# Layer 0's x in a two-layer encoder: turned by PE from its rows, or loaded again in 32-wide blocks and turned by DVE

## The chip, the cores and the metric

The kernel runs on one core of one Trainium2 chip. The metric is the device time of one execution in microseconds. Before the change three runs took 962.6 to 963.75 us, median 963.07. The core has a matrix engine (PE, TensorE), which needs the stationary operand of a product with the contracted index on its 128 partitions; a vector engine (DVE), a scalar engine (ACT), a general engine (POOL), and SP, which here only issues transfers. The transfers run on 16 DMA engines.

## The reference, cut to what matters

x has 256 rows (positions) of 2048 numbers, mem has 256 rows (memory tokens) of 2048. There are two layers. All numbers are float32.

```python
for l in range(2):
    h = rmsnorm(x, norm_g[l])
    proj = h @ w_in[l]                    # 2048 x 7168: gated conv, differential attention, memory attention
    ...
    mn = rmsnorm(mem, mem_norm_g[l])
    mkv = mn @ w_mem_kv[l]                # 2048 x 1024: keys and values of 256 memory tokens
    ...
    y = concatenate([y_a, y_d, y_m], axis=-1) @ w_out[l]    # 2048 x 2048
    x = x + y
```

`rmsnorm` divides a row by the root of its mean square and multiplies by a gain for each of the 2048 columns. The kernel leaves the division to the end of a product (a row's factor can be applied to the result) and applies only the gain to the operand.

## The kernel before, in words

**Products.** `block` computes 256 rows by 512 columns of a product. It walks over the contracted index in 16 slices `k` of 128, two slices to a step. Both operands are split into a leading part and a remainder (`hi` and `lo`), and three products are summed: lines 237, 238 and 239, for each of two row tiles `t`. So a block is 16 x 2 x 3 = 96 matmuls of 128x512. There are 40 blocks: two memory blocks (keys, values) a layer, 14 of `w_in` a layer, 4 of `w_out` a layer.

**Weights.** `load_w` (called by `block` for each step) has SP load two slices of weights, 512 KB, into one of four `raw` buffers (line 210). ACT makes `hi` (line 218, or 221 with a gain) and DVE the remainder `lo` (219, 222), each into one of eight buffers. So weights can be ahead of PE by up to eight slices as `hi` and `lo`, and four more loads as `raw`.

**Operands.** The stationary operand of a block is kept turned, as a tile of 128 partitions by 2 parts by 16 slices by 256 positions. `memT` is the turned mem; `xT` the turned x with the layer's gain. `rows_T` makes two slices at a time: four turns of 128x128 on PE against an identity (line 495; two slices by two row tiles), and `split_T` then has ACT write the leading part (line 200, with the gain as its scale) and DVE the remainder (line 201). `x_rows` is a generator that does this for all 16 slices in eight pieces.

**Order.** The blocks run in this order: memory keys of layer 0, memory values of layer 0, memory keys of layer 1, memory values of layer 1, then the layers themselves. While a block runs, `run_side` takes one piece of side work from a queue of generators after each step. A planner then lays out each engine's instructions from their dependencies and the order in the program; an instruction wrapped in `keep_in_program_order` is held behind whatever its own engine was given before it. Loads of weights and constants are not held in that way.

mem and x share one buffer, `xs`, of rows as they stand in memory. mem is loaded first, and turned while the first block runs (`mem_piece`). During the second block `mem_square` is called before each step's weight load: it takes sums of squares of mem for the row factors, and loads the small constants, among them the gains `norm_g`, which are turned into the columns of `cvb` at its fifth step. In the third block `x_load` brings x into `xs`, 256 columns ahead of each weight load (line 549). In the fourth block `x_rows(xT, 0, ...)` is on the side queue and turns x. The first projection block of layer 0 follows, and needs `xT`. In layer 1, x has been computed on the chip and `x_rows` turns it in the same way.

The pool `keep` has one buffer for each tag; the tags `v`, `ga`, `bgx`, `bgT`, `mqT` and `mga` hold tiles that the layers write later.

Of the kernel before, what the change touches and what calls it, by code (L numbers as in the profile page):

```python
# [10 lines left out]
F32 = mybir.dt.float32  # L11
# [3 lines left out]
ALU = mybir.AluOpType  # L15
# [3 lines left out]
P = 128  # L19
# [4 lines left out]
KT = D_MODEL // P  # L24
# [19 lines left out]
def encoder(ctx: ExitStack, tc: tile.TileContext, x, mem, norm_g, w_in, conv_w, conv_b,  # L44
            dq_g, dk_g, lq1, lk1, lq2, lk2, head_g, mem_norm_g, w_mem_kv, mq_g, mk_g, w_out, out):
    nc = tc.nc
    x, mem, out = x[0], mem[0], out[0]

    def pool(name, bufs, space=None):
        kw = {"space": space} if space is not None else {}  # L50
        return ctx.enter_context(tc.tile_pool(name=name, bufs=bufs, **kw))
# [4 lines left out]
    keep = pool("keep", 1)  # L56
# [8 lines left out]
    def nm(s):  # L65
        uid[0] += 1
        return f"{s}_{uid[0]}"
# [20 lines left out]
    def on_all_rows(v):  # L88
        return v.rearrange("l d -> (l d)").unsqueeze(0).to_broadcast([P, DEPTH * HALF])
# [3 lines left out]
    def load_constants(part):  # L93
        if part is None:
            return
        if part == 0:
            for j, v in enumerate((lq1, lk1, lq2, lk2)):
                nc.sync.dma_start(lam_in[:, j, :], on_all_rows(v))
        else:
            for r0, v in vb_rows[(part - 1) * 4:part * 4]:  # L100
                n, w = v.shape
                for j in range(P // w):
                    nc.sync.dma_start(vb[r0:r0 + n, j * w:(j + 1) * w], v)
# [16 lines left out]
    def g_norm(l, k):  # L120
        return cvb[:, 64 + l * KT + k:65 + l * KT + k]

    def g_mnorm(l, k):
        return cva[:, l * KT + k:l * KT + k + 1]

    cvb = const.tile([P, 96], F32, name="cvb")
# [26 lines left out]
    def rsqrt(t, n):  # L153

        y = small.tile([P, n], F32, tag=f"rs_y{n}", name=nm("rsy"))
        a = small.tile([P, n], F32, tag=f"rs_a{n}", name=nm("rsa"))
        yi = y.bitcast(I32)
        nc.vector.tensor_scalar(yi, t.bitcast(I32), 1, None, ALU.logical_shift_right)
        nc.vector.tensor_scalar(yi, yi, -1.0, float(0x5F3759DF), ALU.mult, ALU.add)
        for _ in range(3):  # L160
            nc.vector.scalar_tensor_tensor(a, y, -0.5, y, ALU.mult, ALU.mult)
            nc.vector.tensor_tensor(a, a, t, ALU.mult)
            nc.vector.scalar_tensor_tensor(y, a, 1.5, y, ALU.add, ALU.mult)
        return y

    side = deque()
# [126 lines left out]
    def col(st, which, t):  # L293
        return st[:, which, t:t + 1]

    def normed(acc, gs, st):

        ng = NB // gs
        ss = small.tile([P, NT, ng], F32, tag=f"ss{ng}", name=nm("ss"))
        for t in range(NT):  # L300
            sq = tmp.tile([P, NB], F32, tag="nat", name=nm("sq"), bufs=4)
            nc.scalar.activation(sq, acc[t], AF.Square)
            nc.vector.tensor_reduce(ss[:, t], sq.rearrange("p (g d) -> p g d", d=gs), AX.X, ALU.add)
            nc.vector.tensor_scalar(ss[:, t], ss[:, t], col(st, R2_64 if gs == HALF else R2_128, t), EPS,
                                    ALU.mult, ALU.add)
        r = rsqrt(ss.rearrange("p t g -> p (t g)"), NT * ng).rearrange("p (t g) -> p t g", t=NT)
        res = []
        for t in range(NT):
            nc.vector.tensor_scalar(r[:, t], r[:, t], col(st, R, t), None, ALU.mult)
            y = tmp.tile([P, NB], F32, tag="nat", name=nm("nat"), bufs=4)  # L310
            nc.vector.tensor_tensor(y.rearrange("p (g d) -> p g d", d=gs),
                                    acc[t].rearrange("p (g d) -> p g d", d=gs),
                                    r[:, t].unsqueeze(2).to_broadcast([P, ng, gs]), ALU.mult)
            res.append(y)
        return res

    def turn(nat, dests):


        for t in range(NT):  # L320
            pt = ps_t.tile([P, NB], F32, tag="t", name=nm("pt"))
            for j in range(NB // P):
                nc.tensor.transpose(pt[:, j * P:(j + 1) * P], nat[t][:, j * P:(j + 1) * P], ident)  # L323
            at = 0
            for dst, h0, nh, gain in dests:
                nc.scalar.activation(dst[:, h0:h0 + nh, t * P:(t + 1) * P],
                                     pt[:, at * P:(at + nh) * P].rearrange("p (h q) -> p h q", h=nh),
                                     AF.Copy, scale=gain)
                at += nh
            yield  # L330
# [159 lines left out]
    def rows_T(dst, src, k, gain=None, n=2):  # L490

        pt = ps_t.tile([P, 2, SEQ], F32, tag="t", name=nm("pt"))
        for j in range(n):
            for t in range(NT):
                nc.tensor.transpose(pt[:, j, t * P:(t + 1) * P], src(k + j, t), ident)  # L495
        for j in range(n):
            split_T(dst, k + j, pt[:, j, :], None if gain is None else gain(k + j))

    def x_rows(dst, l, ks):
        for k in ks:  # L500
            rows_T(dst, lambda k, t: xs[:, t, k * P:(k + 1) * P], k, lambda k: g_norm(l, k))
            yield

    def stats_of(parts, tag):
        ss = small.tile([P, NT], F32, tag="ssum", name=nm("ssum"))
        nc.vector.tensor_reduce(ss, parts, AX.X, ALU.add)
        return row_stats(ss, tag)

    def T_tile(what):
        return big.tile([P, 2, KT, SEQ], F32R, tag="T", name=nm(what))  # L510
# [3 lines left out]
    def x_square(c, t):  # L514
        sq = tmp.tile([P, NB], F32, tag="nat", name=nm("sq"), bufs=4)
        nc.scalar.activation(sq, xs[:, t, c * NB:(c + 1) * NB], AF.Square, accum_out=ssx[:, t, c:c + 1])
# [13 lines left out]

    def mem_square(k):

        load_constants((1, 2, 0, None)[k // 2] if k < 8 else None)
        if k == 8:
            rest_of_constants()
        if k < 8:
            c = k // 2
            for t in range(NT):
                sq = tmp.tile([P, NB], F32, tag="nat", name=nm("sq"), bufs=4)
                tc.keep_in_program_order(  # L540
                    nc.scalar.activation(sq, xs[:, t, c * NB:(c + 1) * NB], AF.Square, accum_out=ssm[:, t, c:c + 1]))

        if k == 10:
            stm.append(stats_of(ssm, "stm"))
            side.append(turn(normed(acc_k, P, stm[0]), [(mkT[0], 0, MH, cvb[:, 56:57])]))

    def x_load(k):
        tc.keep_in_program_order(
            nc.sync.dma_start(xs[:, :, k * P:(k + 2) * P],
                              x[:, k * P:(k + 2) * P].rearrange("(t p) c -> p t c", p=P)))  # L550

    mkT, mv, stm = [], [], []
    for l in range(DEPTH):
        mkT.append(keep.tile([P, MH, SEQ], F32, tag=f"mkT{l}", name=f"mkT{l}"))
        mv.append(keep.tile([P, NT, W_MEM], F32, tag=f"mv{l}", name=f"mv{l}"))
        gm = lambda k: g_mnorm(l, k)
        pinned[0] = l == 0
        acc_k = block(memT, w_mem_kv[l], [(0, NB)], ALLK, gain=gm, before=mem_piece if l == 0 else x_load)
        pinned[0] = False
        if l > 0:  # L560
            side.append(turn(normed(acc_k, P, stm[0]), [(mkT[l], 0, MH, cvb[:, 56 + l:57 + l])]))
            xT = T_tile("xT")
            side.append(x_rows(xT, 0, range(0, KT, 2)))
        acc = block(memT, w_mem_kv[l], [(W_MEM, NB)], ALLK, gain=gm, before=mem_square if l == 0 else None)
        for t in range(NT):
            nc.scalar.activation(mv[l][:, t, :], acc[t], AF.Copy, scale=col(stm[0], R, t))  # L566
    for c in range(4):
        for t in range(NT):
            x_square(c, t)
    flush_side()  # L570

    for l in range(DEPTH):
# [5 lines left out]
        v = keep.tile([P, NT, W_DIFF], F32, tag="v", name=nm("v"))  # L578
        ga = keep.tile([P, NT, W_DIFF], F32, tag="ga", name=nm("ga"))
# [19 lines left out]
        mqT = keep.tile([P, MH, SEQ], F32, tag="mqT", name=nm("mqT"))  # L599
        mga = keep.tile([P, NT, W_MEM], F32, tag="mga", name=nm("mga"))  # L600
# [11 lines left out]
        bgT = None  # L612
# [67 lines left out]
        if l + 1 < DEPTH:  # L680
            xT = T_tile("xT")
# [47 lines left out]
```

## Time and profile before

| | us |
|---|---|
| median of three runs | 963.07 |
| the profiled execution's own time | 962.88 |
| its span | 961.1 |
| PE busy | 953.7 |
| DVE busy | 671.6 |
| ACT busy | 560.6 |

The span is the time from the first to the last instruction. Busy times are sums over an engine's instructions within the span; matmuls are pipelined, so one shows some 0.39 us although they follow one another closer than that. PEld is the load of the stationary operand, which runs beside the matmuls. A row of the lines view gives the line, the engine, the operation, the tiles and their shape, the count, the busy time and mean in ns, and then the idle time before it with what ended it. A row of a window gives for each engine the busy time and count, then the clock of PE as granted (1.00 is full), the mean busy share of the 16 DMA engines, and GB/s. A row of a timeline gives the start, the time to the end of the row's instructions, and what they are; x4 means four merged. The chain of waits gives start, time and what the end of the program hung on at that moment. In the DMA view a line gives packets and bytes of a stretch, and a queue's line the packets, the MB and the time of its packets as a share of 16 engines' time in that stretch.

### The profile page before, as it was taken

The numbers are of one execution on the slowest core, as the hardware profiler recorded it, in microseconds if no ns is written. First come the engines' busy times: TensorE is split into PE (matmuls) and PEld (weight loads), VectorE is DVE, ScalarE is ACT, GpSimd is POOL, SyncE is SP. The second block draws the span as 40 slices with busy tenths as digits, with TensorE's granted clock in tenths as the row PEclk, the third lists the DMA queues.
The fourth block names the chain that finished last, engine by engine and source line by source line (L and its number), as shares of the span: only waits on it lengthen the run. The fifth ranks groups of instructions, "written<-read, shape, count | busy, mean of one in ns | idle before, by whom it ended". The sixth has DMA issues, their size and how long they took to land.

```text
span 961.1 us, 13428 instructions
## 1 busy us (share of the span) xinstructions
PE 953.7 (99%) x4482; PEld 790.4 (82%) x4482; DVE 671.6 (70%) x1496; ACT 560.6 (58%) x1103; POOL 1.4 (0%) x8
## 2 busy tenths in 40 slices
PE   8999999999999999999999999999999999999998
PEld 6888888888888888888888888888888888888886
DVE  5867778865787775567666678856787775568562
ACT  5857656755666655554555556754665655554441
POOL 0000000000000000000000000000000000000000
PEclk9999999999999999999999999999999999999999
DMA  8775565566555555555555665576455555555661
GB/s 267 263 270 181 171 195 178 167 209 195 175 154 167 166 165 161 176 172 178 177 188 184 188 184 177 175 213 194 147 170 176 162 169 165 174 168 176 216 227 58
DMA packets 103530, 175.27 MB, mean 182 GB/s; under 512 B 6318, under 2 KB 29732, under 8 KB 103460
## 3 DMA queue, kind: packets, MB, share of 16 engines
q1 hardware_dynamic: 102116, 173.09, 57.5%
q10 hardware_dynamic: 1344, 1.33, 0.5%
q8 instruction: 35, 0.57, 0.2%
q14 instruction: 35, 0.29, 0.1%
HBM read 172.29 MB, written 2.10 MB: 181 GB/s over the span
## 4 chain that ended last, share of the span: by engine, by line
PE 98%; DMA 1%; DVE 0%; SPq 0%; ACT 0%; issue 0%; DVEq 0%; ACTq 0%
PE acc L237 30%; PE acc L239 30%; PE acc L238 30%; PE po L357 2%; PE pt L495 1%; PE ptT L350 1%; PE s L465 1%; DMA xs<-in_mem_dram 1%; PE s L419 1%; PE s L418 1%; PE ptq L383 1%; PE py L342 0%; PE pt L323 0%; PE pt L638 0%; PE pt L629 0%; DVE lo L222 0%
## 5 line engine op out<-in xcount | busy, mean ns | idle before, releaser
L218 ACT CAST hi<-raw 128x512 fp32r<-128x512 f32 x576 | 355.9, 622 | 318.3 <-PE acc L239 195.3
L219 DVE TENSOR_TENSOR lo<-raw,hi 128x512 fp32r<-128x512 f32 x576 | 394.9, 689 | 203.8 <-ACT hi L218 198.7
L237 PE MATMUL acc<-hi,xT 128*128 128x512 f32 x896 | 353.9, 395 | 0.0
L238 PE MATMUL acc<-lo,xT 128*128 128x512 f32 x896 | 352.2, 393 | 0.0
L239 PE MATMUL acc<-hi,xT 128*128 128x512 f32 x896 | 350.3, 393 | 0.0
L237 PEld LDWEIGHTS acc<-hi,xT 128*128 128x128 f32 x896 | 168.4, 188 | 33.8
L238 PEld LDWEIGHTS acc<-lo,xT 128*128 128x128 f32 x896 | 168.4, 188 | 33.5
L239 PEld LDWEIGHTS acc<-hi,xT 128*128 128x128 f32 x896 | 168.0, 188 | 33.6
L238 PE MATMUL acc<-lo,yT 128*128 128x512 f32 x256 | 99.9, 391 | 0.0
L239 PE MATMUL acc<-hi,yT 128*128 128x512 f32 x256 | 99.2, 390 | 0.0
L237 PE MATMUL acc<-hi,yT 128*128 128x512 f32 x256 | 98.3, 392 | 0.0
L222 DVE SCALAR_TENSOR_TENSOR lo<-raw,cva,hi 128x512 fp32r<-128x512 f32 x64 | 46.2, 748 | 16.2 <-ACT hi L221 15.8
L239 PEld LDWEIGHTS acc<-hi,yT 128*128 128x128 f32 x256 | 48.1, 188 | 9.9
L238 PEld LDWEIGHTS acc<-lo,yT 128*128 128x128 f32 x256 | 48.1, 188 | 9.8
L237 PEld LDWEIGHTS acc<-hi,yT 128*128 128x128 f32 x256 | 48.1, 188 | 9.7
L221 ACT ACTIVATE hi<-raw,cva 128x512 fp32r<-128x512 f32 x64 | 44.0, 721 | 19.4 <-PE acc L239 10.6
L238 PE MATMUL acc<-lo,memT 128*128 128x512 f32 x124 | 48.6, 392 | 0.0
L239 PE MATMUL acc<-hi,memT 128*128 128x512 f32 x124 | 48.4, 390 | 0.0
L237 PE MATMUL acc<-hi,memT 128*128 128x512 f32 x124 | 44.5, 395 | 0.1
L238 PEld LDWEIGHTS acc<-lo,memT 128*128 128x128 f32 x124 | 23.3, 188 | 4.9
L239 PEld LDWEIGHTS acc<-hi,memT 128*128 128x128 f32 x124 | 23.3, 188 | 4.8
L237 PEld LDWEIGHTS acc<-hi,memT 128*128 128x128 f32 x124 | 22.8, 188 | 5.0 <-ACT mv L566 0.5
(154 smaller groups left out, 686.9 us busy)
## 6 DMA issues: line engine op xcount, KB each, us to landing
raw<-in_w_in_dram SPq DMA_DIRECT2D x192, 512.0 KB
raw<-in_w_out_dram SPq DMA_DIRECT2D x64, 512.0 KB
raw<-in_w_in_dram SPq DMA_DIRECT2D x64, 256.0 KB
raw<-in_w_mem_kv_dram SPq DMA_DIRECT2D x31, 512.0 KB
xs<-in_x_dram SPq DMA_DIRECT2D x8, 256.0 KB
xs<-in_mem_dram SPq DMA_DIRECT2D x7, 256.0 KB
out_dram<-xs SPq DMA_DIRECT2D x8, 128.0 KB
out_dram<-xs ACTq DMA_DIRECT2D x8, 128.0 KB
```

The source lines that it names most:

```text
L218: nc.scalar.copy(hi, raw[:, j])
L219: nc.vector.tensor_tensor(lo_, raw[:, j], hi.bitcast(F32), ALU.subtract)
L221: ins = [nc.scalar.activation(hi, raw[:, j], AF.Copy, scale=gains_of(j)), nc.vector.scalar_tensor_tensor(lo_, raw[:, j], gains_of(j), hi.b ...
L222: nc.vector.scalar_tensor_tensor(lo_, raw[:, j], gains_of(j), hi.bitcast(F32), ALU.mult, ALU.subtract)]
L237: nc.tensor.matmul(acc[t], sh, hi, start=first, stop=False)
L238: nc.tensor.matmul(acc[t], sh, lo, start=False, stop=False)
L239: nc.tensor.matmul(acc[t], sl, hi, start=False, stop=last)
L350: nc.tensor.transpose(pt[:, k, i * P:(i + 1) * P], e[:, i, k * P:(k + 1) * P], ident)
L357: nc.tensor.matmul(po[:, i, :], eT[:, k, i * P:(i + 1) * P], v[:, k, h * P:(h + 1) * P], start=k == 0, stop=k == NT - 1)
L383: nc.tensor.transpose(pt[:, j, :], nat[t][:, j * P:(j + 1) * P], ident)
L418: nc.tensor.matmul(s[c][:, i, :], qi, k_first(yT, c, h), start=True, stop=False)
L419: nc.tensor.matmul(s[c][:, i, :], qi, k_second(yT, k2, c, h), start=False, stop=True)
```

## The change

x is brought in a second time, for layer 0's `xT` alone. `x_blocks(k)` is called at the start of `mem_square(k)`, so before each of the eight weight loads of layer 0's memory values. Each call issues four DMAs on SP, held in program order: 32 positions by 2048 columns of x are cut into runs of 32 columns, and DMA number `a` puts every fourth run onto partitions 32a to 32a+31. There are four tiles `pieces` of 64 positions each, in buffers that are free at that time. `x_turned(xT)` goes on the side queue after that block. For each piece DVE turns all 32x32 squares in one instruction, multiplies by the gain (broadcast along the positions), ACT copies the result into the leading part, and DVE subtracts for the remainder. Layer 0's `x_rows`, with its PE turns, is gone. The load of x into `xs` stays, since the row sums and the residual need it. `xT` is allocated one block earlier.

```diff
     def mem_square(k):
 
+        x_blocks(k)
         load_constants((1, 2, 0, None)[k // 2] if k < 8 else None)
...
+    B, PT = 32, 2
+    pieces = [keep.tile([P, PT, KT, B], F32, tag=tag, name=nm("xb")) for tag in ("v", "ga", "bgx", "bgT")]
+
+    def x_blocks(k):
+        i = k // 4
+        for t, a in ((k % 4 // 2, a) for a in range(P // B)):
+            rows = x[(i * PT + t) * B:(i * PT + t + 1) * B].rearrange("c (k a r) -> a c k r", a=P // B, r=B)
+            tc.keep_in_program_order(nc.sync.dma_start(pieces[i][a * B:(a + 1) * B, t], rows[a]))
+
+    def x_turned(dst):
+        gain = cvb[:, 64:64 + KT].unsqueeze(2).to_broadcast([P, KT, PT * B])
+        for i, y in enumerate(pieces):
+            f = keep.tile([P, KT, PT * B], F32, tag=("mqT", "mga")[i % 2], name=nm("xf"))
+            nc.vector.transpose(f.rearrange("p k (t c) -> p t k c", c=B), y)
+            yield
+            nc.vector.tensor_tensor(f, f, gain, ALU.mult)
+            ts = slice(i * PT * B, (i + 1) * PT * B)
+            nc.scalar.copy(dst[:, 0, :, ts], f)
+            yield
+            nc.vector.tensor_tensor(dst[:, 1, :, ts], f, dst[:, 0, :, ts].bitcast(F32), ALU.subtract)
+            yield
...
+        else:
             xT = T_tile("xT")
-            side.append(x_rows(xT, 0, range(0, KT, 2)))
         acc = block(memT, w_mem_kv[l], [(W_MEM, NB)], ALLK, gain=gm, before=mem_square if l == 0 else None)
...
+        if l == 0:
+            side.append(x_turned(xT))
```

## The prediction

> **What bounds the kernel now.** I read the page's head and chain first, to see which engine an edit must relieve.
>
> ```profile
> PE 953.7 (99%) x4482; PEld 790.4 (82%) x4482; DVE 671.6 (70%) x1496; ACT 560.6 (58%) x1103; POOL 1.4 (0%) x8
> ...
> PE 98%; DMA 1%; DVE 0%; SPq 0%; ACT 0%; issue 0%; DVEq 0%; ACTq 0%
> ```
>
> PE is the chain. A PE instruction that goes is worth its own issue time, as long as the weights still arrive ahead of PE. So I next looked for the turns of x (line 495, the chain of waits in order of time), for the pace of PE around one of them (timeline of PE), and for the pace of a stretch without turns (the chain again).
>
> ```profile
> 92.29 0.44 PE pt L495 x4
> ...
> 119.97 0.44 PE pt L495 x4
> ```
>
> ```profile
> 110.17 0.60 PE L495 MATMUL pt<-ident,xs 128*128 128x128 f32 x4
> 110.52 0.71 PE L239 MATMUL acc<-hi,xT 128*128 128x512 f32 x2
> 111.07 0.40 PE L237 MATMUL acc<-hi,xT 128*128 128x512 f32 x1
> ...
> 112.00 0.62 PE L239 MATMUL acc<-hi,xT 128*128 128x512 f32 x2
> 112.46 0.40 PE L237 MATMUL acc<-hi,xT 128*128 128x512 f32 x1
> ```
>
> ```profile
> 46.80 0.45 PE acc L237 x2
> 48.16 0.45 PE acc L237 x2
> ...
> 53.66 0.67 DVE lo L222
> 54.33 0.68 ACT mv L566
> 55.06 0.50 PE acc L237
> ```
>
> There are eight groups of four turns, one at 92.29 and seven up to 119.97, all on the chain. The first matmul pair with its group takes 111.07 - 110.17 = 0.90 us, without one 112.46 - 112.00 = 0.46: 0.44 us a group. One k takes PE 48.16 - 46.80 = 1.36 us (six matmuls), so a step of two k's, which is one weight load of 512 KB, takes 2.72. The first layer's second memory block (call it V0) has eight steps and ends just before 55.06, where the next block (K1) starts; its last step must have its weights at about 52.0.
>
> Then the loads of that stretch, since the new DMAs go there: SP's timeline, ACT's timeline, and the windows of ten us (PE, PEld, DVE, ACT, POOL, clock, DMA share, GB/s).
>
> ```profile
> 18.46 0.90 SPq L210 DMA_DIRECT2D raw<-in_w_mem_kv_dram  x2
> ...
> 20.11 0.37 SPq L210 DMA_DIRECT2D raw<-in_w_mem_kv_dram  x1
> ...
> 22.93 0.37 SPq L210 DMA_DIRECT2D raw<-in_w_mem_kv_dram  x1
> ...
> 38.22 0.37 SPq L210 DMA_DIRECT2D raw<-in_w_mem_kv_dram  x1
> 38.68 0.42 SPq L549 DMA_DIRECT2D xs<-in_x_dram  x1
> ```
>
> ```profile
> 23.99 1.34 ACT L221 ACTIVATE hi<-raw,cva 128x512 fp32r<-128x512 f32 x2 [0.34 <-DMA raw<-in_w_mem_kv_dram]
> ...
> 46.84 0.73 ACT L221 ACTIVATE hi<-raw,cva 128x512 fp32r<-128x512 f32 x1 [0.50 <-PE acc L239]
> ```
>
> ```profile
> 20.00:30.00 10.00, 10.00 (x50) 8.17 (x49) 6.95 (x17) 7.32 (x17) 0.00 (x0) 1.00 0.80 266
> 30.00:40.00 10.00, 10.00 (x46) 8.28 (x45) 8.30 (x16) 10.00 (x23) 0.00 (x0) 1.00 0.76 251
> 40.00:50.00 10.00, 10.00 (x46) 8.29 (x45) 8.11 (x21) 6.78 (x12) 0.00 (x0) 1.00 0.87 302
> 50.00:60.00 10.00, 9.90 (x44) 7.86 (x44) 7.95 (x31) 4.39 (x7) 0.00 (x0) 1.00 1.03 364
> 60.00:70.00 10.00, 10.00 (x50) 8.36 (x49) 6.35 (x9) 7.38 (x12) 0.00 (x0) 1.00 0.48 157
> 70.00:80.00 10.00, 10.00 (x46) 8.29 (x45) 6.35 (x11) 6.60 (x10) 0.00 (x0) 1.00 0.63 214
> ```
>
> V0's weights are issued from 20.11 to 38.22 and its last are needed at 52.0: a lead of 14 us, which at 46.84 shows as ACT waiting for PE to free a buffer. This lead is the cover for everything the change puts on SP's queue. But the DMA engines are already 0.76 to 1.03 busy from 20 to 60.
>
> **The change part by part.** *Off PE:* eight groups at 0.44 are 3.5 us; matmuls beside a group also run slightly slower than the 1.36 us pace (the pair takes 0.46 against 0.45), for some 0.3 more. Gain 3.8 us. The ACT and DVE work behind the turns goes too, but both had slack there.
>
> *On DVE and ACT.* These groups give the prices:
>
> ```profile
> L201 DVE SCALAR_TENSOR_TENSOR xT<-pt,cvb,xT 128x256 fp32r<-128x256 f32 x32 | 15.0, 479 | 2.6 <-ACT xT L200 2.1
> ...
> L200 ACT ACTIVATE xT<-pt,cvb 128x256 fp32r<-128x256 f32 x32 | 14.5, 471 | 5.5 <-PE pt L495 4.3 <-DVE xT L201 1.2
> ...
> L425 DVE TENSOR_REDUCE mx<-e 128x4 f32<-128x1024 f32 x12 | 14.6, 1213 | 0.1
> ```
>
> Half of L201 (7.5 us of DVE) and half of L200 (7.2 us of ACT) go. In come four pieces of 128x1024, each a turn, a multiply and a subtract on DVE and a copy on ACT. At 1.21 us for 1024 elements that is 14.6 us of DVE, and under 5 of ACT. No turn on DVE is in the trace; two passes instead of one would make it 2.4 us, a half pass 0.6, so 4 turns are 2.4 to 9.6; I take 1.21, the row of the same shape. One of the twelve DVE operations is emitted after each step, so eight fall into K1 (55 to 78). DVE is busy there 0.5x7.95 + 6.35 + 0.8x6.35 = 15.4 us of 22.7; with 8x1.21 it is 25.1, 2.4 too many where no lead is left. With lead, or where they slip into V0, nothing. I take 1.0, from 0 to 5.
>
> *On SP and the DMA engines.* 32 DMAs of 64 KB, four ahead of each V0 weight load, pinned there. SP pays 32x0.42 = 13 us of issue; a step needs five issues, 2.1 us, below 2.72, so issue alone costs nothing. Each DMA is 32 partitions by 16 runs of 128 B: 16384 packets, 1024 for each of 16 engines. What a 128 B packet costs is the open number, since none is in the trace. The nearest rows, from the DMA view in windows 2 to 3, 12 to 14, 16.47 to 16.6, 24 to 26 and 30 to 32 us (packets, MB, share of 16 engines):
>
> ```profile
> DMA packets 462, 0.24 MB, mean 235 GB/s; under 512 B 33, under 2 KB 452, under 8 KB 462
> q1 hardware_dynamic: 404, 0.20, 70.1%
> ...
> DMA packets 728, 0.70 MB, mean 349 GB/s; under 512 B 47, under 2 KB 728, under 8 KB 728
> q1 hardware_dynamic: 728, 0.70, 110.3%
> ...
> q1 hardware_dynamic: 2, 0.00, 0.9%
> ...
> DMA packets 376, 0.73 MB, mean 364 GB/s; under 512 B 21, under 2 KB 21, under 8 KB 376
> q1 hardware_dynamic: 376, 0.73, 101.9%
> ...
> DMA packets 430, 0.20 MB, mean 102 GB/s; under 512 B 42, under 2 KB 426, under 8 KB 430
> q1 hardware_dynamic: 430, 0.20, 45.6%
> ```
>
> The two that move no data take 0.009x16x0.13/2 = 9.4 ns each. Taking the small ones off at that price: 512 B cost (11.2 - 0.3)/371 = 29.4 ns in the first window and (14.6 - 0.4)/388 = 36.6 in the last (the four 64 KB lam loads); 1 KB cost 51, 2 KB 91. A line from 1 KB through 512 B gives 13 ns for 128 B, one from 9.4 to 29.4 gives 14.3, the same for the lam loads, the nearest in form (64 KB, issued in a row by SP), 14.3x36.6/29.4 = 17.8. Ends: 9.4, and 29.4 if nothing is saved below 512 B. I take 18, the nearest in form.
>
> *The sum.* The two weight loads issued at 18.46 and the one before are through the engines at about 23.1 (1.5 MB at 364 GB/s from 18.3, with a slow start of 0.5; an estimate). Behind them come eight weight loads, 256x91/16 = 1.45 us each, 11.6; the lam loads, 1.1; and 1.024x18 = 18.4 us of blocks. The last weights of V0 have left the engines at 54.2. A tail follows: the load issued at 18.46 should be through at 21.6 and was waited for until 23.99, 2.4 us. Then ACT and DVE each take 0.7 before PE has both halves: 58.0 against 52.0, so PE is 6.0 us late. K1 brings 256 KB of x and 512 KB of weights a step, 256x51/16 + 1.45 = 2.3 us against 2.72, and adds no lateness. Sum: 6.0 + 1.0 - 3.8 = +3.2 on the profiled execution's 962.88, which lies 0.2 below the median of 963.07: 966.1, say 966. SP's later loads wait behind these; they keep what lead they had.
>
> A page of the Trainium skill, DMA: Bandwidth & Descriptors, speaks both ways. In "Specifications" it says that below 512 B a transfer no longer runs at line rate, because of a read-modify-write; in "Why small descriptors are slow" that a packet costs a cycle for each 32 B and some three more. By the first nothing is saved below 512 B and the sum is that of the third rival below; by the second, 128 B take 7/19 of 512 B, 10.8 ns as an estimate, and the sum is that of the first. On the sizes that the trace has, the second gives 19 : 35 : 67 and the rows 29 : 51 : 91, so it is near them; no row is below 512 B but the empty ones.
>
> **The rivals.** *Covered (faster).* Lateness is 1.024 us for each ns of packet price, so it is nothing at 12 ns or less. Then the time is 962.9 - 3.8 = 959.1, with a little for DVE 959.4. For it: 13 ns by the large packets, and a quarter of 29.4 is 7.4. Against it: the lam loads, shorter packets cost more per byte in every row, and no idle engine stretch in 20 to 60 to catch up in.
>
> *Break-even.* Between 13 and 16.7 ns the stall and the 3.8 us cancel to within 0.2%, about what a measurement of this kernel can tell from no change (1.9 us): 961.1 to 965.0. Two of my three lines point there. Against it: it is a narrow window, and a DVE without lead pushes it out upwards.
>
> *Nothing saved below 512 B.* At 29.4 ns the last V0 weights are 17.7 us late: 962.9 + 17.7 + 1.0 - 3.8 = 977.8. For it: 36.6 ns for 512 B in the lam loads; against it: the empty packets at 9.4, so a packet has no large fixed price.
>
> *The change does less than it says:* the blocks may be moved, but PE's turns of x in layer 0 are gone from the program and each block is pinned behind a weight load; I give this no chance of its own.
>
> **How the numbers follow.** Covered 0.30, break-even 0.25, stall above the gain (17 to 27 ns, 965 to 975) 0.33, nothing saved 0.12. Forecast 966, the third of these. Faster 0.30, same 0.25, slower 0.33 + 0.12 = 0.45. Range 959.0 to 975.5: the whole of the first three cases, without most of the last.
>
> **What would show it.** No line 495 between 55 and 130, and 96 matmuls in 21.8 us in the first projection block. Packets in 20 to 60 rise by 16900 with a DMA share near 1, and the price can be read from a stretch of them. PE idle before line 237 or 238 in V0, released by hi or lo, those by a DMA of raw: 6 us in all, growing over its steps. Wrong if that idle is under 1 us (packets cheap), if it is over 12 us (packets dear), or if it lies in K1 behind DVE's turns.

## The result, and the profile after

The changed kernel takes 979.17 us (median of four runs, 978.14 to 980.63) against 963.03 for the kernel before in the same comparison: a ratio of 1.0167, with a 95% interval from 1.0152 to 1.0182. It is 16.1 us slower, where 3 were forecast. The profiled execution's span grew from 961.1 to 977.8 us.

The page of the changed kernel, in the order in which the page of before was read: busy times and the chain's shares.

```profile
PE 957.4 (98%) x4450; PEld 790.3 (81%) x4450; DVE 679.4 (69%) x1492; ACT 557.5 (57%) x1091; POOL 1.4 (0%) x8
...
PE 93%; DMA 2%; DVE 2%; issue 1%; ACT 1%; SPq 1%; DVEq 0%; ACTq 0%
```

PE has lost the 32 turns (4482 matmuls before, 4450 now). The chain of what ended last lay on PE for 98% of the span and now does for 93%. The waits between 18 and 140 us (who <- releaser: us in total, times, longest) say where PE stands idle.

```profile
PEld acc L237 <- ACT mv L591: 9.8, 1, 9.8
PE acc L237 <- ACT mv L591: 9.4, 1, 9.4
...
PE acc L238 <- DVE lo L222: 5.1, 5, 2.0
DVE xf L568 <- DMA xb<-in_x_dram: 4.0, 1, 4.0
ACT mv L591 <- DVE stm L284: 3.0, 1, 3.0
DVE xf L568 <- DMA raw<-in_w_mem_kv_dram: 2.2, 1, 2.2
...
DVE xf L568 <- DMA lam_in<-in_lambda_q_dram: 1.0, 1, 1.0
```

There are two kinds. Five waits for `lo`, 5.1 us together, look like the late weights that the prediction looked for; DVE's timeline below shows what the two longest of them stood behind. One wait of 9.4 us, for `mv`, was not in its sum. `mv` is the evacuation of V0's result out of PSUM (the memory that PE sums into) by ACT, which multiplies by the row factors `stm`. K1 gets its two accumulators only when it is done: the pool has four, and the other two still hold the result of layer 0's memory keys, which DVE reads only at 75.62 (line 311). Four rows around K1's start, first of before (timelines of DVE, ACT and PE), then of the changed kernel:

```profile
53.22 0.17 DVE L284 COPY stm<-rsy 128x2 f32<-128x2 f32 x1
...
54.32 1.37 ACT L566 ACTIVATE mv<-acc,stm 128x512 f32<-128x512 f32 x2
...
54.57 0.39 PE L239 MATMUL acc<-hi,memT 128*128 128x512 f32 x1
55.06 0.50 PE L237 MATMUL acc<-hi,memT 128*128 128x512 f32 x1
```

```profile
72.33 0.17 DVE L284 COPY stm<-rsy 128x2 f32<-128x2 f32 x1
...
72.54 1.27 ACT L591 ACTIVATE mv<-acc,stm 128x512 f32<-128x512 f32 x2 [3.02 <-DVE stm L284]
...
63.52 0.39 PE L239 MATMUL acc<-hi,memT 128*128 128x512 f32 x1
73.28 0.79 PE L237 MATMUL acc<-hi,memT 128*128 128x512 f32 x1 [9.37 <-ACT mv L591]
```

V0's last matmul comes at 63.52 instead of 54.57, 8.95 us late. Of these, 4.67 had come about before V0 started: the block ahead of it, layer 0's memory keys (call it K0), has its last matmul at 37.48 instead of 32.81 in PE's timeline. Then K1's first matmul is 73.28 - 55.06 - 8.95 = 9.3 us later still, because `stm` came at 72.33 instead of 53.22. Why `stm` is so late stands in DVE's timeline (turns, some of the remainders between them, and the row-factor instructions):

```profile
30.43 1.25 DVE L568 STREAM_TRANSPOSE xf<-xb 128x1024 f32<-128x1024 f32 x1 [3.96 <-DMA xb<-in_x_dram]
31.59 0.71 DVE L222 SCALAR_TENSOR_TENSOR lo<-raw,cva,hi 128x512 fp32r<-128x512 f32 x1
...
48.98 1.25 DVE L568 STREAM_TRANSPOSE xf<-xb 128x1024 f32<-128x1024 f32 x1 [2.21 <-DMA raw<-in_w_mem_kv_dram]
50.15 1.18 DVE L574 TENSOR_TENSOR xT<-xf,xT 128x1024 fp32r<-128x1024 f32 x1
51.32 0.74 DVE L222 SCALAR_TENSOR_TENSOR lo<-raw,cva,hi 128x512 fp32r<-128x512 f32 x1
...
57.09 1.24 DVE L568 STREAM_TRANSPOSE xf<-xb 128x1024 f32<-128x1024 f32 x1
...
58.88 0.16 DVE L158 TENSOR_SCALAR rsy<-stt 128x2 int32<-128x2 int32 x1
...
66.76 1.41 DVE L222 SCALAR_TENSOR_TENSOR lo<-raw,cva,hi 128x512 fp32r<-128x512 f32 x2 [0.68 <-ACT hi L221]
```

The planner put all four turns ahead of `stm`, the first into K0 and three into V0, although the side queue gets them only after V0. Each turn needs a piece of x that comes in through the loaded queue, and what the planner put behind a turn on DVE waits with it: 3.96 us of waiting at 30.43, 2.21 at 48.98, 1.01 in between. (For two of the three the profile names another transfer of the queue, weights or constants; a turn reads nothing but its piece, so that it waited for the piece there is inferred.) The remainders `lo` of the weights stand behind the turns. PE's first stop, 1.79 us in K0, ends at 32.36 and its longest, 1.97, at 52.12 in V0, just behind the remainders of 31.59 and 51.32. So these two are turns that waited, not weights that came late. Then the chain of small instructions that makes `stm` (its root is begun at 58.88) is interleaved with the other work on the turned pieces and with remainders of K1's weights, some of which wait for `hi` and so for K1's own transfers. Up to `stm`, DVE was given 37 remainders of weights in the kernel before and 40 here; K0 and V0 need 32. So `stm` stands behind eight slices of K1's weights here (five before), and K1 can't start before those have come.

The clock adds to it. A window of 1 us after K1's start and the one of ten us (columns as before: engines, granted clock, DMA share, GB/s), and then PE's timeline:

```profile
73.00:74.00 1.00, 0.72 (x2) 0.63 (x3) 0.83 (x6) 0.80 (x2) 0.00 (x0) 0.50 0.94 335
```

```profile
78.99 0.47 PE L238 MATMUL acc<-lo,memT 128*128 128x512 f32 x1
79.30 0.39 PE L239 MATMUL acc<-hi,memT 128*128 128x512 f32 x1
79.53 0.40 PE L237 MATMUL acc<-hi,memT 128*128 128x512 f32 x1
```

After the idle 9.4 us the granted clock is 0.50. From 73.28 to 78.99 thirteen matmuls start, nearly all 0.43 us apart; from 79.30 they are 0.23 apart again. Thirteen times 0.23 is 3.0 of these 5.7 us, so 2.7 are lost. The account of the span: 8.95 (K0 and V0) + 9.3 (K1's start) + 2.7 (clock) - 3.8 (PE's turns, as predicted) = 17.1, against 16.7 measured.

### The profile page after: what moved, and what is told of

It reads as the page before. It is cut to its first block, busy times and chain, and to the rows that moved or that the text cites. A ratio compares the mean times of both kernels' runs of the same rounds, so it can differ in the third digit from the quotient of the medians.

```text
span 977.8 us, 13393 instructions
## 1 busy us (share of the span) xinstructions
PE 957.4 (98%) x4450; PEld 790.3 (81%) x4450; DVE 679.4 (69%) x1492; ACT 557.5 (57%) x1091; POOL 1.4 (0%) x8
## 4 chain that ended last, share of the span: by engine, by line
PE 93%; DMA 2%; DVE 2%; issue 1%; ACT 1%; SPq 1%; DVEq 0%; ACTq 0%
PE acc L237 28%; PE acc L239 28%; PE acc L238 28%; PE po L357 2%; DVE lo L222 1%; PE ptT L350 1%; DMA xb<-in_x_dram 1%; DMA raw<-in_w_mem_kv_dram 1%; PE s L465 1%; SPq L562 1%; PE s L419 1%; PE s L418 1%; PE pt L495 1%; PE ptq L383 1%; PE acc L265 0%
```

## The experiments

### The turns held in their place, and the loads without the turns

The first kernel keeps each turn behind what DVE was given before it in the program, so that none can slip into V0.

```diff
-            nc.vector.transpose(f.rearrange("p k (t c) -> p t k c", c=B), y)
+            tc.keep_in_program_order(nc.vector.transpose(f.rearrange("p k (t c) -> p t k c", c=B), y))
```

> The four DVE turns are held in program order on DVE, so they stand behind the row factors stm instead of ahead of them; loads as in the changed kernel. Theory A (late data on an in-order DVE: turns and lo's that wait for late DMAs stand ahead of stm, stm frees the value block's PSUM through mv, and PE starts the next block late and at a lower clock): the 9.4 us wait before the third block falls under 1 us, the slow matmuls behind it go, and the time is 963 to 969. Theory B (the short packets alone make the weights late, DVE's order does not matter): 977 or more. Theory C (DVE has too much work): 975 to 980, since the work is the same.

Measured: 971.91 us, ratio 1.0085 (1.0068 to 1.0101), 7.3 us better than the change, and in none of the three ranges. K1's start (ACT's timeline, then PE's):

```profile
64.28 1.33 ACT L221 ACTIVATE hi<-raw,cva 128x512 fp32r<-128x512 f32 x2 [0.74 <-DMA raw<-in_w_mem_kv_dram]
65.52 1.24 ACT L591 ACTIVATE mv<-acc,stm 128x512 f32<-128x512 f32 x2
...
66.24 0.79 PE L237 MATMUL acc<-hi,memT 128*128 128x512 f32 x1 [2.87 <-ACT mv L591]
```

`stm` is ready at 53.96, close to the 53.22 of the kernel before, and the turns run from 64.55 on. Still PE waits 2.87 us for `mv`, which now stands on ACT: ACT too was given four leading parts `hi` of K1's weights ahead of it, and these wait for transfers. So the gate before K1 has two keepers, DVE with `stm` and ACT with `mv`.

The second puts PE's turns of x back and leaves the loads, which nothing reads.

```diff
-        else:
             xT = T_tile("xT")
+            side.append(x_rows(xT, 0, range(0, KT, 2)))
...
-            side.append(x_turned(xT))
```

> The 32 block loads stay, but nothing reads them: layer 0's x is turned by PE as before. Theory A: PE waits some 5 us in the value block for late weights, and a few more where stm stands behind late lo's: 966 to 973. Theory B: the whole loss, and PE's turns on top: 980 to 984. Theory C: 963 to 964, as before the change.

Measured: 971.05 us, ratio 1.0074 (1.0059 to 1.0089), 7.4 us for the loads alone, within theory A's range. The waits between 18 and 140 us:

```profile
ACT hi L221 <- DMA raw<-in_w_mem_kv_dram: 15.1, 11, 2.7
...
PE acc L237 <- ACT hi L221: 4.3, 5, 1.8
```

This is the lateness that was predicted: leading parts wait for `raw`, PE for them, five times, all in V0. PE's timeline has V0's last matmul here:

```profile
62.91 0.39 PE L239 MATMUL acc<-hi,memT 128*128 128x512 f32 x1
```

That is 62.91 - 54.57 = 8.3 us late, for 4.3 us of idle time in the list. The list counts from the end of a matmul that is shown as 0.39 us long where the next would follow after 0.23, and PE's timeline has the four starts behind each stop 0.33 to 0.45 apart; pauses too short to be listed add to it.

### Longer runs, and the turns without the loads

The third loads the same bytes in runs of 2 KB.

```diff
-            rows = x[(i * PT + t) * B:(i * PT + t + 1) * B].rearrange("c (k a r) -> a c k r", a=P // B, r=B)
-            tc.keep_in_program_order(nc.sync.dma_start(pieces[i][a * B:(a + 1) * B, t], rows[a]))
+            rows = x[(i * PT + t) * B:(i * PT + t + 1) * B, a * NB:(a + 1) * NB]
+            to = pieces[i][a * B:(a + 1) * B, t].rearrange("c k r -> c (k r)")
+            tc.keep_in_program_order(nc.sync.dma_start(to, rows))
```

> The 32 loads bring the same bytes as whole runs of 512 columns, 2 KB packets in place of 128 B (so x is turned wrongly and the result is not the reference's). 1024 packets at 91 ns instead of 16384 at 16.5 are 5.8 us of the 16 engines instead of 16.9. Theory A: the lead covers it, 959 to 963. Theory B: 959 to 962. Theory C: 972 or more.

Measured: 978.51 us, ratio 1.0153 (1.0137 to 1.0168), no better than the change by what these runs can tell, and in theory C's range (DVE has too much work) alone. The first turn (DVE's timeline) and K1's start (PE's):

```profile
31.47 1.25 DVE L569 STREAM_TRANSPOSE xf<-xb 128x1024 f32<-128x1024 f32 x1 [8.17 <-DMA raw<-in_w_mem_kv_dram]
...
73.80 0.79 PE L237 MATMUL acc<-hi,memT 128*128 128x512 f32 x1 [7.95 <-ACT mv L592]
```

The same two waits are there without a packet of 128 B in x's second load. The bulk of what made the kernel slow does not hang on how x is cut.

The fourth has the turns and no loads; the pieces are filled with ones by POOL at the start, so layer 0's operand is that of a constant.

```diff
-        x_blocks(k)
...
+    for y in pieces:
+        nc.gpsimd.memset(y, 1.0)
```

> No block loads: POOL fills the four tiles with ones at the start, and DVE and ACT do the same work on them (layer 0's projections are those of a constant x). What DVE's work costs by itself. Theory A: the gain of PE's turns alone, 959 to 961. Theory B: 959. Theory C: 970 or more.

Measured: 968.20 us, ratio 1.005 (1.0035 to 1.0065). No theory had this: without a single transfer more, the turns alone cost 4.6 us where 4 should have been won. Again a line of PE's timeline:

```profile
61.73 0.79 PE L237 MATMUL acc<-hi,memT 128*128 128x512 f32 x1 [6.47 <-ACT mv L593]
```

The turns now wait for no transfer. The planner put two of them at the very start and two into V0, with all the work behind them (DVE is busy for all of 30 to 50 us); V0 ended 0.3 us late, but `stm` came at 60.78, behind 40 remainders as in the change. Loads alone 7.4 and turns alone 4.6 make 12.0; the change costs 16.1. The 4 us between would be the turns' waits for late data, which neither half has; that is argued from the difference alone.

### Moving the row factors ahead: a device that only moved the wait

The next four hold the first remainder that follows `stm` in the program behind `stm` (a "hold"), so that K1's weights can't come before it.

```diff
+                if hold_lo[0]:
+                    tc.keep_in_program_order(ins[1])
+                    hold_lo[0] = False
...
             stm.append(stats_of(ssm, "stm"))
+            hold_lo[0] = True
+        if k == 12:
```

With turns and no loads, and with the whole change:

> As the run with turns alone (no block loads, tiles filled by POOL), but the next lo after the row factors is held behind them on DVE, so stm comes after 26 lo's and not after 40. Theory D (two separate losses: the loads make weights late, and the planner's DVE order puts stm behind turns and behind lo's of the next block): the wait of 6.5 us and the slow matmuls behind it go, 959 to 961. Theory C (DVE, full from 30 to 60 us, has no time for the turns there): 965 to 969 as before this edit.

> The changed kernel with the same hold and nothing else: stm after 26 lo's, the turns where the planner puts them. Theory D: the wait before the third block falls under 2 us and the late weights stay: 966 to 972. Theory C: 975 or more.

Measured: 968.79 us, ratio 1.0057 (1.004 to 1.0074), and 981.85 us, ratio 1.0194 (1.0179 to 1.021); both lie in theory C's range and not in D's. PE's timeline of the first:

```profile
54.13 0.79 PE L242 MATMUL acc<-lo,memT 128*128 128x512 f32 x1 [6.04 <-DVE lo L223]
```

`stm` came early, at 52.97 in the first, but the turns' work stood ahead of it, and the remainders of V0 that are held behind `stm` came late instead. PE waited 6.04 us inside V0 for what it had waited 6.47 for at its end. The device is no test of the gate.

The next spreads the loads (two DMAs a step in V0, one in K1, two in the first steps of the fourth block), with held turns and the hold; the one after it has held turns, the hold and 2 KB runs.

```diff
+    todo = deque((i, t, a) for i in range(len(pieces)) for t in range(PT) for a in range(P // B))
+
+    def x_some(n):
+        for _ in range(n):
+            i, t, a = todo.popleft()
...
     def mem_square(k):
-        x_blocks(k)
+        x_some(2)
...
     def x_load(k):
+        x_some(1)
```

> The 32 block loads spread over three blocks (two a step, then one, then two), the turns held in program order, stm held ahead as above. Each step then brings under 2.8 us of transfers for 2.72 us of PE. Theory D: both losses go, 959 to 962, faster than before the change. Theory C: 966 or more. If the late weights do not come from the blocks' time on the DMA engines but from their number on SP, 965 to 970.

> All loads in the value block as in the change, but as runs of 2 KB (x is turned wrongly), turns and stm held as in the spread version. If the weights were late because of the short packets: 959 to 963. If because of the number of DMAs on SP or their bytes: 967 to 972, as with the short packets and the turns held.

Measured: 966.81 us, ratio 1.0039 (1.0024 to 1.0054), and 968.18 us, ratio 1.0051 (1.0036 to 1.0066). The first lies outside D's range and in C's, the second where the number of DMAs on SP or their bytes would put it (967 to 972). Both still have a wait for `mv` before K1, 5.42 and 3.89 us, and while that gate stands, their times do not tell what the transfers cost. By its ranges alone, theory C, too much work for DVE, has fitted four of the runs so far; the next are the test of it.

### Taking the gate away

`mv` holds K1 up only because K1's accumulators are V0's. Two PSUM banks of another pool lie idle there. With them, K1 can start before `mv` is done; nothing is reordered by hand.

```diff
-        acc = [ps_acc.tile([P, NB], F32, tag="acc", name=nm("acc")) for _ in range(NT)]
+        where, tag = (ps_s, "s") if idle else (ps_acc, "acc")
+        acc = [where.tile([P, NB], F32, tag=tag, name=nm("acc")) for _ in range(NT)]
...
-        acc_k = block(memT, w_mem_kv[l], [(0, NB)], ALLK, gain=gm, before=mem_piece if l == 0 else x_load)
+        acc_k = block(memT, w_mem_kv[l], [(0, NB)], ALLK, gain=gm, before=mem_piece if l == 0 else x_load,
+                      idle=l == 1)
```

This was put into the change, into the turns without loads, into spread loads with held turns (without the hold), and into the kernel before as a control.

> The changed kernel, but the third block sums into the two PSUM banks that only the attention uses later, so PE need not wait for mv to start it. Theory E (the weights' lead is no cover for the start of the third block: the planner put stm and mv behind eight slices of the third block's lo and hi, so PE starts it only when these are there): the wait of 9.4 us and the slow matmuls behind it go, the waits inside the value block (some 5 us) stay, 965 to 970. Theory F (the bank is not what counts; PE would run out of weights at that point anyway): 975 or more.

> Turns alone (no block loads, tiles filled by POOL) with the same two banks. Theory E: 959 to 961, the gain of the removed PE turns and no loss. Theory C (DVE has no time for the turns): 966 to 969 as without the banks.

> Block loads spread over three blocks, turns held in program order on DVE, the two banks; stm no longer held ahead of lo's, as that made PE wait in three runs. Theory E: 959 to 962, below the kernel before. Theory F: 965 or more, since the DMA engines are full from 20 to 80 us.

> The kernel before with the two banks and nothing else, as the control for the three others: 962 to 963.5; its wait for mv is 0.5 us.

Measured, against 963.15 for the kernel before:

| | us | ratio (95%) |
|---|---|---|
| the change with the banks | 970.40 | 1.0078 (1.0065 to 1.0091) |
| turns without loads, with the banks | 958.70 | 0.9953 (0.994 to 0.9966) |
| spread loads, held turns, banks | 967.22 | 1.0037 (1.0023 to 1.0051) |
| kernel before with the banks | 962.72 | 0.9996 (0.9987 to 1.0005) |

Theory E's ranges are met to within 0.4 us by the first two and missed by the third; the fourth is as expected. The control shows that the banks by themselves are worth nothing that these runs can tell: in the kernel before, `mv` was in time. In the change they are worth 979.2 - 970.4 = 8.8 us. In the turns without loads they are worth 968.2 - 958.7 = 9.5 us, and the turns on DVE now win 4.4 us. Waits and a window of that kernel:

```profile
PE acc L239 <- DVE lo L222: 0.2, 1, 0.2
```

```profile
30.00:40.00 10.00, 9.77 (x44) 7.76 (x43) 10.00 (x15) 10.00 (x22) 0.00 (x0) 1.00 0.73 233
40.00:50.00 10.00, 10.00 (x45) 7.99 (x44) 10.00 (x16) 7.97 (x15) 0.00 (x0) 1.00 0.57 189
```

DVE is busy every moment from 30 to 50, as without the banks, and PE hardly waits, though `stm` comes even later (66.53). So the amount of DVE work was not the trouble; what hung behind it was.

The change with the banks still waits in K0 and V0. Its waits, and its first turn in DVE's timeline:

```profile
PE acc L239 <- DVE lo L222: 6.8, 4, 4.7
```

```profile
32.26 1.25 DVE L569 STREAM_TRANSPOSE xf<-xb 128x1024 f32<-128x1024 f32 x1 [6.99 <-DMA xb<-in_x_dram]
```

One turn, in K0, waits 6.99 us for its piece and PE 4.7 us for the remainder behind it. The spread loads, expected near the turns' full gain, missed it. The first and the last of seven windows:

```profile
20.00:30.00 10.00, 10.00 (x49) 8.17 (x48) 6.76 (x17) 6.13 (x14) 0.00 (x0) 1.00 1.01 232
...
80.00:90.00 10.00, 8.32 (x33) 5.55 (x31) 7.83 (x18) 5.29 (x8) 0.00 (x0) 1.00 0.97 242
```

The DMA share stays between 0.94 and 1.12 in all seven, from 20 to 90 us, and PE starts 49 matmuls in the first and 33 in the last: there is no slack stretch to spread into, since K1, too, brings x and weights. (Around 90 us, 2.13 us are a wait for DVE, line 312, and not for weights.) Its twelve runs lie between 962.55 and 970.58 us, far wider than those of the kernel before.

### The loads alone, by packet size

What stays open is how much of the rest is the turns' waiting, the short packets, and the bytes. With the banks and held turns, the programs with 128 B and with 2 KB runs differ in the length of the runs alone. Two things go with it: SP issues a block of long runs faster (0.42 us against 0.63, below), and the planner's order is not the same (the first turn stands at 66.74 behind `stm` with the short runs, at 59.97 ahead of it with the long ones). The third kernel makes 2 KB runs compute the reference: with them, slice `k` of layer 0's contraction holds columns 512a + 32k + r instead of 128k + p, so the rows of `w_in[0]` and the gain are loaded in that order, each weight load as four DMAs of 32 partitions.

```diff
+            for a in range(4):
+                to = raw[a * 32:(a + 1) * 32]
+                for g in range(len(cols)):
+                    src = quarters[a * NB:(a + 1) * NB][:, cols[g][0]:cols[g][0] + n]
...
+                    nc.sync.dma_start(to[:, :, g * n:(g + 1) * n], src[rows:rows + CK * 32].rearrange("(j r) c -> r j c", r=32))
```

> The changed kernel's loads (128 B runs), the turns held in program order, the third block in the two idle PSUM banks. What is left should be late weights alone. Theory G (the 16384 short packets hold the DMA engines too long): 966 to 970. Theory H (the number of DMAs on SP or the bytes): 966 to 970 too; the next run tells the two apart.

> The same with runs of 2 KB in the same number of DMAs and bytes (x is turned wrongly, so the result is not the reference's). Theory G: 959 to 962. Theory H: 966 to 970, as with the short runs.

> The same 2 KB runs made right: in layer 0 the slice k of the contracted index is the columns 512a + 32k + r, so the rows of w_in are loaded in four quarters of 32 partitions a step, and the gain likewise. Theory G, and SP's four issues of some 0.4 us a step hidden under 2.72 us of PE: 959 to 962, below the kernel before; the two blocks with split columns need eight issues a step, and if that shows 963 to 970. Theory H: 966 or more.

Measured, against 963.31: 965.83 us, ratio 1.0038 (1.0022 to 1.0053), with 128 B; 961.56 us, ratio 0.9982 (0.9973 to 0.9991), with 2 KB; 961.83 us, ratio 0.9982 (0.9973 to 0.9991), for the one with strided slices, the last two as theory G had it. The five runs of the first fall into two groups, 965.29 to 965.83 and 968.6 to 969.35, and its profile is that of the slowest; so its median and its ratio lie 1.1 us apart. Waits of the first, then of the second:

```profile
ACT hi L221 <- DMA raw<-in_w_mem_kv_dram: 23.8, 14, 3.1
...
PE acc L238 <- ACT hi L221: 4.9, 5, 1.7
```

```profile
ACT hi L221 <- DMA raw<-in_w_mem_kv_dram: 12.9, 11, 2.5
...
PE acc L238 <- ACT hi L221: 1.1, 2, 0.8
```

The same weights wait half as long, and PE's wait falls from 4.9 to 1.1 us; V0 takes 30.69 us in the first profile and 23.89 in the second, 21.53 in the kernel before. The short runs cost 965.8 - 961.6 = 4.3 us by the medians (5.4 by the ratios) once the gate and the turns' waiting are gone. The last kernel computes what the reference does and is faster than the kernel before by 0.18% (0.09 to 0.27). It is a small gain, and its interval lies partly within 0.2%.

The steps down from the change, each with the ones above it in place:

| what is taken away | us left | step |
|---|---|---|
| (the change) | 979.2 | |
| the gate before K1 (banks) | 970.4 | -8.8 |
| the turns' waiting ahead of the weights' remainders (held) | 965.8 | -4.6 |
| the short runs (2 KB runs) | 961.6 | -4.3 |
| the loads themselves (turns without loads, planner's place) | 958.7 | -2.9 |

The order of the steps matters for their sizes: 2 KB runs as the first step gave 0.7, as the third 4.3; held turns as the first gave 7.3, as the second 4.6. The runs come from different comparisons, whose kernel before lay between 963.0 and 963.6, and by the intervals of the ratios a step is known to some 2 us; by the ratios the second and third are 3.9 and 5.4.

## Why the prediction was right or wrong

*The gain on PE* was put at 3.8 us. The turns without loads, with the banks, won 4.4 us; the control with the banks alone 0.4 (0.04%, within -0.05 to 0.13). That is right.

*The price of a 128 B packet* was put at 18 ns. A step of its working misread a row: of the 388 packets in the stretch of the lam loads, four are not 512 B long ("under 2 KB 426, under 8 KB 430"). The trace keeps the time of each packet, and the 384 of 512 B took 32.8 ns there, not 36.6; with that, 14.3x32.8/29.4 is 16.0 and not 17.8. The DMA view of the loads alone, from 24 to 56 us:

```profile
DMA packets 19323, 6.17 MB, mean 193 GB/s; under 512 B 16959, under 2 KB 17471, under 8 KB 19319
...
q1 hardware_dynamic: 19319, 6.13, 97.7%
```

Taking the longer packets off at the prediction's prices would leave 18 ns for a short one. But the long packets are dearer here. The trace has the times of these 19,323 packets: the mean is 15.7 ns for 128 B (16,261 packets), 59.9 for 512 B and 111.6 for 2 KB. Over all 16,384 short packets the mean is 15.7 ns here and 14.7 in the changed kernel, the median 13 in both. At 14.7 to 15.7 the prediction's own terms end in break-even, so its direction owes something to what it left out.

The Trainium skill, DMA: Bandwidth & Descriptors, says in "Specifications" that a transfer below 512 B no longer runs at line rate, and the trace agrees: a 128 B packet at 14.7 ns moves 8.7 bytes a ns, one of 512 B at the prediction's 29.4 ns 17.4. What the prediction made of it, that nothing is saved below 512 B, the trace does not bear out: the short packet took half the time. The Trainium skill, on the same page in "Why small descriptors are slow", has the count of cycles from which 10.8 ns was estimated; the measured price is above it.

*The lateness of V0's weights* was put at 6.0 us. In the loads alone V0 ended 8.3 us late and the time rose by 7.4; with the banks and held turns the 128 B loads cost 965.8 - 958.7 = 7.1. The mechanism is right and the size some 1 to 2 us low, but its parts make up for each other. In the loads alone from 24 to 56 us the blocks' packets took 15.7 ns and not 18, which is 2.4 us less; the weights' packets of 2 KB took 111.6 and not 91, 2.6 us more for eight weight loads; those of the lam loads 59.9 and not 36.6, 0.7 more. Another part shows in SP's timeline of the changed kernel:

```profile
38.14 2.58 SPq L562 DMA_DIRECT2D xb<-in_x_dram  x4
...
52.69 1.15 SPq L210 DMA_DIRECT2D raw<-in_w_mem_kv_dram  x1
```

Four blocks took SP 2.58 us, 0.64 each and not 0.42, and with 0.56 or more for the weights a step needs 3.1 us of issue, above the 2.72 that PE takes. "Issue alone costs nothing" was therefore wrong as argued. Whether SP or the transfers themselves set the pace is not separated: V0's last weights went out at 52.69 instead of 38.22, with SP and the DMA engines both busy nearly all the time until then. The picture of the wait as growing over the steps in V0 does not fit the whole change either: there 4.67 of the 8.95 us came about in K0, and V0 ran late in a few jumps, the largest of them behind a turn that waited for data.

*DVE*: a turn was bounded by 0.6 and 2.4 us and taken at 1.21. The group of the changed kernel has it so:

```profile
L568 DVE STREAM_TRANSPOSE xf<-xb 128x1024 f32<-128x1024 f32 x4 | 5.0, 1243 | 7.2 <-DMA xb<-in_x_dram 4.0 <-DMA raw<-in_w_mem_kv_dram 2.2 <-DMA lam_in<-in_lambda_q_dram 1.0
```

The price was right; the 7.2 us at the end of the row were not thought of. Here the prediction failed, in the step "I take 1.0, from 0 to 5", and in the sentence before it, "With lead, or where they slip into V0, nothing". They did slip into V0, the first even into K0. DVE's work was counted as busy time against room, when what mattered was the order: which instruction stands behind the turns, and who waits for it. Behind them stood the remainders of K0's and V0's weights, then `stm`, on which `mv` and all of K1 hang. The wait it named as its falsifier, "if it lies in K1 behind DVE's turns", was the one that came, and the upper end of 5 us was worked out from busy time, not from that wait. The banks measured the gate at 8.8 us, the held turns their waiting at 4.6: some 13.4 us for a term of 1.0. With both gone 965.8 - 963.3 = 2.5 us are left, where the rest of the prediction's sum is 6.0 - 3.8 = 2.2.

*The lead of 14 us* was called "the cover for everything the change puts on SP's queue". It was not free time. In the kernel before, DVE and ACT have `stm` and `mv` in line behind slices of K1's own weights (five for `stm`); those come early enough only because of the lead. With loads and turns in the way, not just the weights came late but also the small chain behind them; in the turns without loads that chain alone did, and it cost 9.5 us.

*The rivals.* 977.8 us, "nothing saved below 512 B", came within 1.4 us of the result and was wrong as a mechanism: the packets took 14.7 ns, and with 2 KB runs the change still took 978.5. "Covered" needed 12 ns or less and a DVE that hides; with the gate gone, held turns and 2 KB runs 961.6 was reached, with no loads 958.7.

What else stays open: the last 2.9 us of the ladder mix the loads' bytes with the place of the turns (held in one kernel, the planner's in the other); no run separates them.

## What to carry to other kernels

When work is put on an engine that is in order and "has room", find the instruction that stands behind it and ask who waits for that; a row factor of 0.2 us that frees an accumulator can cost more than all the work put in. An operation that waits for a transfer hands its wait to everything behind it on its engine, so place it by when its data come, not by when the engine is idle. Prefetched work that is queued ahead of such a small chain makes the prefetch lead a condition and not a reserve; a second pair of accumulator banks took the condition away here at no cost that the control shows.

## What the runs showed of the hardware

After 9.4 us without a matmul the granted clock was 0.50, and it took 5.7 us of matmuls (73.28 to 78.99) until they were 0.23 us apart again. Elsewhere the slow stretch was 3.2 us long after 2.87 us without a matmul (turns held), 5.3 after 6.47 (turns without loads) and 6.1 after 6.04 (the same with the hold), so its length does not simply follow the pause. Waits of 1 to 2 us inside V0 left the clock at 1.00 in the windows of ten us of the changed kernel and of the loads alone. In the 128 B loads with held turns and banks they did not: after waits of 1.2 and 1.7 us the three windows of 1 us from 47 to 50 have 0.50. The Trainium skill, TensorE: Matmul & The Clock Gate, "Part 1: The HAM clock gate", has half rate after an idle window of some 3.4 us and full rate after some 3.4 us of work; the half rate agrees, but it came after shorter pauses, too, and the way back took between 3.2 and 6.1 us.

A DVE turn of 128x1024 float32 in 32x32 squares took 1243 ns, hardly more than a multiply of the same shape (1219 ns): here turning was no dearer than a pass. A 128 B packet took 14.7 ns of an engine against 29.4 for 512 B in the prediction's first window: a quarter of the bytes for half of the time. From 24 to 56 us a 2 KB packet took 92.8 ns on the mean in the kernel before, 111.6 with the short-run loads alone and 109.8 with the 2 KB runs, held turns and banks; more transfers made it dearer, whatever their packets. And SP took half as long again to issue 64 KB in runs of 128 B as in runs of 2 KB (the blocks of the changed kernel, then of the 2 KB runs with held turns and banks; least, median and longest in ns):

```profile
L562 SPq DMA_DIRECT2D xb<-in_x_dram x32: 565/625/858, 19.8 to 52.0; - x32
...
L564 SPq DMA_DIRECT2D xb<-in_x_dram x32: 310/420/1342, 19.6 to 48.9; - x32
```
